# Moving the accumulating weight-sum transfers from the recurrence to the up projections, with new places for casts and low parts

## The chip, the cores and the metric

The kernel runs on one core of a Trainium2 chip. TensorE (PE) multiplies matrices into PSUM, VectorE (DVE) and ScalarE (ACT) do the elementwise work, GpSimd (POOL) does a little of it and issues transfers, SyncE (SP) issues most transfers. Each engine works through its own instructions in order, and waits for the others by semaphores. The metric is the device time of one execution in microseconds (us); the time before is the median of three runs.

## The reference, cut to what matters

A trunk of two layers on 1024 tokens of width 1024, all in float32. Layer 0 mixes tokens by a gated linear recurrence with 8 heads of 128, layer 1 by attention in a window of 128. After each mixer, and after each feed-forward part, comes a layer norm of the residual sum.

```
q, f, i, g = split(h @ w_in, 4)                  # layer 0, per head of 128
fg = lb + (1 - lb) * sigmoid(f)
S_t = diag(fg_t) S_{t-1} + (1 - fg_t) i_t^T ;  o_t = S_t^T silu(q_t)
o = o * rsqrt(mean(o^2) + eps) * g_norm_w * silu(g) ;  mix = o @ w_out
h = layer_norm(alpha * h + mix)
u = causal_depthwise_conv3(h @ ffn_w_in) + conv_b    # both layers, 2 x 2816 columns
a, b = split(u, 2) ;  h = layer_norm(alpha * h + (silu(a) * b) @ ffn_w_out)
```

## The kernel before, in words

**Products.** Every large matrix product is done with operands split into a high part (a cast by ACT to a reduced float32 format) and a low part (what is left, by DVE; `low_part`, L193), in three matmuls of 512 columns (`mm3`, L218 to L220). The largest products are cut into 2 x 2 blocks and done with seven block products instead of eight (numbers 1 to 7 in the code), so that sums and differences of weight blocks are needed beside the weights.

**The order of the work.** `Order` (`od`) keeps an account in us: `od.t` is what PE has been given so far, `od.v` what DVE has. Tasks are Python generators, which `od.tick()` steps when their time in `od.t` has come; `od.fill` lets DVE have one more job as long as `od.v` is under `od.t + od.room`, and `od.hook` issues casts. Costs are guesses written into the calls (`cost=0.03` for a small matmul; `mm3` adds 3 x 512 / 2365 us). In the recurrence the order of PE, SP, ACT, DVE and POOL is the order of these calls (`manual_schedule`). Elsewhere, as in the up projection, only PE's order is so fixed; a planner orders the other engines, each instruction as its operands and its buffer come free, earlier lines first.

**The recurrence** (`recur`, one generator per head). While PE runs the 98 block products of the later heads' q, f, i and g (`product(n)`, L1368 on: 12 matmuls of 512 columns, in four quarters k), the head in hand goes through its levels: DVE updates qp and kp by halves of blocks (`update`, L1083 to L1088), ACT keeps a copy for the next level (`stash`, L1070 and L1071), and PE computes the scores of a level in bursts of small tiles (`scores`, `blocks`, `column_sums`, all L224). Then come transposes of kp and of the values, the states St, the output, and `norm`: squares with sums by ACT (L1197), mean and power by POOL (L1198, L1199), the scaling by DVE into og (L1201), 8 transposes of og by PE (L228).

**Weights in the recurrence.** `raw` tiles are loaded by SP two pairs ahead. For the block products 6 and 7, and 5 and 4, DVE first makes sums in place (jobs "a", L1290 and L1291, and "b", L1293 and L1294). `cast_next` (called by the hook) issues ACT's cast of the next block (L1271) once the sums it needs have been issued to DVE; `job_next` issues DVE's low part at least 1 us of the account after the cast. A block product goes into one of four PSUM banks; before it, the bank's earlier result must have been read (`evacuate`, ACT L1346 to L1352 and DVE L1358).

**Weight sums of the down projections.** Both down projections use four sums of blocks of `ffn_w_out` (`bsd`, in device memory). They are made by transfers alone, issued by POOL: plain copies (L1225) and copies that add to what is there (`accum_op`, L1226). For each layer there are four groups of rows (3, 3, 3 and 2 x 128 of them), of eight transfers each, partly one behind the other; 64 transfers in all. `product(n)` takes one from the list ahead of each of the first 64 block products.

**The start.** x blocks are turned by PE (`x_pair`, L228) and DVE makes sums of their parts (`sums_of_x`, L822 to L825). `last_sums` (L845) casts more of them later.

**Convolution parameters.** `conv_params` waits until 330 in the account, loads them by ACT, has PE turn four pieces (L964), each into a new psax tile (there are two) from which DVE copies (L965).

**The up projection** (`Up.run`). For each of 22 blocks fc of 2 x 128 columns: four loads by SP (L466), casts, sums (L475 to L478) and low parts, seven block products, and `collect`: their sums, the convolution (L521, L523), the gate (L526, L528) and a store to `gd` (L529). The multiplication of L528 is POOL's for fc 0 and 1, DVE's for the rest. The down projection reads `gd`, `ffn_w_out` and, from its third block product on, `bsd`; POOL does the power of each layer norm (L267).

Of the kernel before, what the change touches and what calls it, by code (L numbers as in the profile page):

```python
# [16 lines left out]
P = 128  # L17
# [4 lines left out]
BL = 32  # L22
NH = 8
FF = 2816
NF = FF // P
# [29 lines left out]
class Order:  # L55
# [40 lines left out]
    def tick(self):  # L96
        for task in sorted(self.chains, key=lambda k: k[0]):
            if task[0] <= self.t:
                self.step(task)
        if self.hook:  # L100
            self.hook()
        while self.fill and self.v < self.t + self.room and self.fill():
            pass

    def finish(self, tasks):
# [25 lines left out]
def trunk(ctx: ExitStack, tc: tile.TileContext, a: dict, out: bass.AP):  # L131
    nc = tc.nc
    PS = bass.MemoryType.PSUM
    od = Order()
# [32 lines left out]
    def psax():  # L167
        return axp.tile([P, 1024], F32, name="psax")
# [222 lines left out]
    sub, add = ALU.subtract, ALU.add  # L391
# [7 lines left out]
    class Up:  # L399
# [97 lines left out]
        def collect(self, p, fc, ps):  # L497
# [18 lines left out]
            if p in (4, 3):  # L516
# [10 lines left out]
                else:  # L527
                    (nc.gpsimd if fc < 2 else nc.vector).tensor_tensor(ca, ca, c, op=ALU.mult)  # L528
                    nc.sync.dma_start(gd[:, fc, :], ca)  # L529

        def run(self, ready, down):

            od.finish(ready[:4])
# [12 lines left out]
            for fc in range(2):  # L546
                self.collect(7, fc, self.product(7, fc, mm[2 + fc]))
                self.collect(4, fc, ax[fc])
                self.collect(5, fc, ax[2 + fc])
            self.weights(2)  # L550
            for fc in range(2):
                self.collect(3, fc, self.product(3, fc, mm[fc]))
            banks, n = mm[2:] + ax[:2] + mm[:2] + ax[2:], 0
            for fc in range(2, NF):
                if fc > 2:
                    self.weights(fc)
                for p in (1, 2, 6, 7, 4, 5, 3):
                    self.collect(p, fc, self.product(p, fc, banks[n % 8]))
                    n += 1
                    if fc == NF - 1 and p in (1, 6, 4):  # L560
                        down.ahead.append(down.operands(0, len(down.ahead)))

# [139 lines left out]
    with tc.tile_pool(name="t", bufs=1, reuse_waits="tile") as raws, hgrn_pool as hp:  # L702
# [148 lines left out]
        with tc.tile_pool(name="ep", bufs=1, reuse_waits="tile") as ep:  # L851
# [33 lines left out]
            with tc.manual_schedule(engines={EN.PE, EN.SP, EN.Activation, EN.DVE}):  # L885
# [60 lines left out]
                od.finish([ahead])  # L946
                w0["q"] = qf_split(raws0["q"])
                nc.vector.tensor_copy(msk, mf)
                late = [od.spawn(x_pair(6), 1.0)]

        def conv_params():
            yield 330.0
            for l in range(2):
                crs = []
                for k in range(2):
# [4 lines left out]
                        nc.scalar.dma_start(crs[k][44 * j:44 * (j + 1), :], src.rearrange("(c p) -> c p", p=P))  # L960
                yield 10.0
                for k, cr in enumerate(crs):
                    ps = psax()
                    nc.tensor.transpose(ps[:, :88], cr, ident[:88, :88])  # L964
                    nc.vector.tensor_copy(cwt[:, l, 2 * k:2 * k + 2, :],  # L965
                                          ps[:, :88].rearrange("p (a b) -> p a b", a=2))
                    yield 3.0

            rb = hp.tile([32, 16], F32, name="rb")
            nc.scalar.dma_start(rb, a["rel_bias"])  # L970
# [42 lines left out]
        def recur(h, qs, fg, kp):  # L1013
# [19 lines left out]
            def scores(i, pv, K, Q):  # L1033
# [4 lines left out]
                for c in range(NB):  # L1038
                    for b in range(P // BL):
                        o, g = b * BL, c * (P // BL) + b  # L1040
                        mm32(pv[o:o + BL, c], K[:, g * BL:(g + 1) * BL], second(qv, m)[:, g], cost=0.03,
                             tile_position=(0, o))

                def put():
# [69 lines left out]
            column_sums(sums1, r1, 16)  # L1114
            column_sums(sums2, r2.rearrange("p j b u -> p (j b u)"), 16)
            puts = [scores(2, chunks(ps[:, 384:512]), early, early), scores(3, chunks(ps[:, 768:896]), kp, qp)]
            update(3)
            early = stash(4, hp.tile([P, S], F32, name="kd"))
            place(Ab, 0, chunks(sums0))
# [9 lines left out]
            yield wait  # L1129
            pv = chunks(psax())  # L1130
            low, high = scores(4, pv[:, :, :16], early, early), blocks(5, pv, kp, qp)
            update(5)
            early = stash(6, hp.tile([P, S], F32, name="kd"))
            low()
# [27 lines left out]
            for c in range(NB - 1):  # L1162
                cs = slice(c * P, (c + 1) * P)
                mm32(ps[:, cs], kd[:, cs], V[:, c, :])
            St = hp.tile([P, NB, P], F32, name="St")
            for c in range(NB - 1):
                pc = ps[:, c * P:(c + 1) * P]
# [49 lines left out]
            if h < NH - 2:  # L1217
                nc.sync.dma_start(hod[h], G)

        def weight_sums(l, k0, k1):  # L1220

            w, rows, lower = a["ffn_w_out"][l], slice(k0 * P, k1 * P), slice(FF // 2 + k0 * P, FF // 2 + k1 * P)
            b11, b12, b21, b22 = w[rows, :512], w[rows, 512:], w[lower, :512], w[lower, 512:]
            t1, t2, t3, t4 = [t[rows, :] for t in bsd[l]]
            plain = lambda to, src: lambda: nc.gpsimd.dma_start(to, src)  # L1225
            onto = lambda to, src: lambda: nc.gpsimd.dma_start(to, src, accum_op=add)  # L1226
            return [plain(t3, b22), plain(t1, b11), onto(t3, b12), onto(t1, b12),
                    plain(t2, t3), onto(t2, b11), plain(t4, t2), onto(t4, b21)]

        groups = [weight_sums(l, k0, k1) for l in range(2) for k0, k1 in ((0, 3), (3, 6), (6, 9), (9, 11))]  # L1230
        sums = [one for i in range(0, 8, 4) for four in zip(*groups[i:i + 4]) for one in four]
# [7 lines left out]
        raw_of, landing, cast, low_made, summed_w = {}, {}, {}, set(), set()  # L1239
# [18 lines left out]
        def cast_next(force=False):  # L1258
# [6 lines left out]
                return False  # L1265
            if p in (6, 7) and (m, "a") not in summed_w or p in (5, 4) and (m, "b") not in summed_w:
                return False
            if (m, 0) not in raw_of or p == 3 and (m, 1) not in raw_of or not force and landing[m] > od.t:
                return False
            order_hi.pop(0)  # L1270
# [8 lines left out]
        def job_next(force=False):  # L1279
# [4 lines left out]
            if p in ("a", "b"):  # L1284
# [7 lines left out]
                else:  # L1292
                    tt(b21, b21, b11, op=sub)  # L1293
                    tt(b11, b22, b11, op=sub)  # L1294
                summed_w.add((m, p))
                od.vec(1.4, 0.0)
            else:
                if force:
                    while (m, p) not in cast:
# [69 lines left out]
        def product(n):  # L1369

            m, p = line[n]
            ensure(min(n + 2, len(line) - 1))
            if sums:
                sums.pop(0)()
            b = {2: 1, 5: 2, 3: 2}.get(p, 3 * (m % 2))
            ps = banks[b]
            if b in readers:
# [2 lines left out]
                    od.step(t)  # L1380
            w = home(n)
            for k in range(4):
                mm3(ps, lambda j: w[:, j, k * P:(k + 1) * P], lambda j: moving[p](j, k), k == 0 and p in (1, 2, 5), k == 3, onto=p in (6, 7, 3, 4))
                od.tick()
            done[0] = n + 1
# [42 lines left out]
        with tc.manual_schedule(engines={EN.PE, EN.SP, EN.Activation, EN.DVE, EN.Pool}):  # L1428
# [56 lines left out]
            if sums or jobs or order_hi:  # L1485
# [382 lines left out]
```

## Time and profile before

| | |
|---|---|
| median of 3 runs | 2229.71 us (2228.83 to 2230.94) |
| the profiled execution, its time | 2228.37 us |
| its span, first to last instruction | 2226.6 us |
| PE busy, of the span | 2116.6 us (95%) |
| DVE busy | 1779.9 us (80%) |
| ACT busy | 970.7 us (44%) |
| POOL busy | 185.0 us (8%) |
| mean granted clock of PE | 0.975 |
| transfers by POOL's queue: bytes, share of 16 engines' span | 46.16 MB, 9.8% |
| transfers by SP's queue | 238.26 MB, 32.9% |

The recurrence reaches from about 58 us to 578 us of the span, the first up projection to about 1069 us; the second one ends about 2001 us into it. Busy times are sums over instructions; issuing a transfer or waiting is not counted as busy. The ends of matmuls are modelled, so a busy PE is not PE at its full rate: the granted clock says how fast it was let run, 1.00 being full speed. A row of the timeline gives the start and the length in us, the engine, the line, the operation and its operands (out, then in), and in brackets the idle time ahead of it with what ended it; a row of the waits gives the engine that waited, what it waited for, the total in us, how often, and the longest.

### The profile page before, as it was taken

How to read it: one execution, taken by the hardware profiler on the slowest of the kernel's cores; microseconds unless marked ns; L12 is line 12 of the kernel's file. 1: busy time of each engine (PE TensorE's matmuls, PEld its weight loads, DVE VectorE, ACT ScalarE, POOL GpSimd, SP SyncE). 2: the span in 40 equal slices, each digit the busy share in tenths (PEclk: the TensorE clock that was granted, in tenths of full speed). 3: DMA queues.
4: the chain of work that ended last, by engine and by line, in shares of the span. 5: the costliest groups of instructions: out<-in, count | busy, mean ns of one | idle time of the engine just before them, and what ended most of it. 6: DMA issues, size and time to landing. Idle time of an engine off the chain costs nothing.

```text
span 2226.6 us, 31496 instructions
## 1 busy us (share of the span) xinstructions
PE 2116.6 (95%) x12303; PEld 1759.3 (79%) x12303; DVE 1779.9 (80%) x2422; ACT 970.7 (44%) x1562; POOL 185.0 (8%) x214
## 2 busy tenths in 40 slices
PE   8796978799999999999999999999999999999998
PEld 7675766577777888888888888888888888888887
DVE  5564645567599999998898767897999999988986
ACT  5453444355244444444442336672444444444430
POOL 2012112000011000000000112340100000000001
PEclk9898988899999999999999999999999999999999
DMA  8158878415222322222875441204223222239762
GB/s 271 26 103 204 205 133 201 94 50 169 74 102 85 105 85 78 84 86 95 283 261 189 161 132 34 56 26 155 104 81 99 85 86 85 78 124 308 244 203 107
DMA packets 239789, 286.80 MB, mean 129 GB/s; under 512 B 30184, under 2 KB 160408, under 8 KB 239384
## 3 DMA queue, kind: packets, MB, share of 16 engines
q1 hardware_dynamic: 223328, 238.26, 32.9%
q0 software_dynamic: 15456, 46.16, 9.8%
q8 instruction: 97, 1.59, 0.3%
q10 hardware_dynamic: 856, 0.37, 0.1%
q14 instruction: 52, 0.43, 0.1%
HBM read 241.72 MB, written 89.15 MB: 149 GB/s over the span
## 4 chain that ended last, share of the span: by engine, by line
PE 78%; issue 10%; DVE 5%; DMA 3%; POOL 2%; ACT 2%; SPq 0%; DVEq 0%; POOLq 0%; ACTq 0%
PE psmm L218 15%; PE psmm L220 15%; PE psmm L219 14%; PE psax L218 9%; PE psax L220 9%; PE psax L219 9%; DMA bsd<-bsd 2%; PE psax L224 2%; PE psmm L228 1%; PE psmm L224 1%; PE psax L1642 1%; POOL bsd L1226 1%; PE psax L228 1%; PE psmm L1493 1%; DVE HL L193 0%
## 5 line engine op out<-in xcount | busy, mean ns | idle before, releaser
L218 PE MATMUL psmm<-T,HL 128*128 128x512 f32 x768 | 307.6, 401 | 17.8 <-DVE VG L1358 12.3
L220 PE MATMUL psmm<-T,HL 128*128 128x512 f32 x768 | 302.0, 393 | 3.0 <-DVE HL L193 3.0
L219 PE MATMUL psmm<-T,HL 128*128 128x512 f32 x768 | 301.8, 393 | 0.0
L523 DVE SCALAR_TENSOR_TENSOR Y<-Y,cwt,Y 128x1023 f32<-128x1023 f32 (+1 forms) x176 | 225.2, 1281 | 45.5 <-ACT Y L521 43.9
L245 ACT CAST HL<-rx 128x1024 fp32r<-128x1024 f32 (+1 forms) x151 | 151.6, 1007 | 181.8 <-PE psmm L219 40.2
L193 DVE TENSOR_TENSOR HL<-rx,HL 128x1024 fp32r<-128x1024 f32 (+1 forms) x151 | 176.4, 1174 | 19.3 <-ACT HL L245 19.1
L218 PEld LDWEIGHTS psmm<-T,HL 128*128 128x128 f32 x768 | 146.5, 191 | 48.2 <-DVE VG L1358 12.7
L220 PEld LDWEIGHTS psmm<-T,HL 128*128 128x128 f32 x768 | 145.5, 189 | 35.2 <-DVE HL L193 4.2
L219 PEld LDWEIGHTS psmm<-T,HL 128*128 128x128 f32 x768 | 146.3, 191 | 29.2 <-DVE T L193 0.5
L267 POOL TENSOR_TENSOR rs<-rs,nhalf 128x1 f32<-128x1 f32 x32 | 44.9, 1402 | 1295.5 <-DVE rs L266 1295.4
L521 ACT ACTIVATE Y<-Y,cwt 128x1024 f32<-128x1024 f32 x88 | 108.8, 1237 | 96.1 <-DVE Y L510 85.7
L218 PE MATMUL psax<-T,HL 128*128 128x512 f32 x352 | 137.3, 390 | 0.0
L219 PE MATMUL psax<-T,HL 128*128 128x512 f32 x352 | 137.0, 389 | 0.0
L220 PE MATMUL psax<-T,HL 128*128 128x512 f32 x352 | 136.9, 389 | 0.0
L193 DVE TENSOR_TENSOR HL<-raw,HL 128x512 fp32r<-128x512 f32 (+1 forms) x121 | 93.1, 788 | 31.5 <-ACT HL L1271 18.6
L218 PE MATMUL psmm<-HL 128*128 128x512 f32 x220 | 88.2, 401 | 8.6 <-ACT qs L1348 7.3
L1271 ACT CAST HL<-raw 128x512 fp32r<-128x512 f32 x98 | 55.2, 619 | 91.8 <-DVE raw L1291 62.8
L245 ACT CAST HT<-rx 128x1024 fp32r<-128x1024 f32 (+1 forms) x37 | 35.5, 961 | 127.2 <-DVE rx L477 83.7
L220 PE MATMUL psmm<-HL 128*128 128x512 f32 x220 | 87.1, 396 | 0.0
L219 PE MATMUL psmm<-HL 128*128 128x512 f32 x220 | 87.1, 396 | 0.0
L220 PEld LDWEIGHTS psax<-T,HL 128*128 128x128 f32 x352 | 66.2, 188 | 13.8
L219 PEld LDWEIGHTS psax<-T,HL 128*128 128x128 f32 x352 | 66.1, 188 | 13.6
(392 smaller groups left out, 5393.2 us busy)
## 6 DMA issues: line engine op xcount, KB each, us to landing
rx<-in_ffn_w_in_dram SPq DMA_DIRECT2D x136, 256.0 KB, 3.2
rx<-gd SPq DMA_DIRECT2D x118, 256.0 KB, 3.8
bsd<-in_ffn_w_out_dram POOLq DMA_DIRECT2D x36, 768.0 KB, 7.9
gd<-Y SPq DMA_DIRECT2D x44, 512.0 KB, 2.6
raw<-in_hgrn_w_in_dram SPq DMA_DIRECT2D x30, 512.0 KB, 5.4
rx<-in_ffn_w_out_dram SPq DMA_DIRECT2D x54, 256.0 KB, 4.6
R<-bsd SPq DMA_DIRECT2D x44, 256.0 KB, 5.1
Y<-in_ffn_w_in_dram SPq DMA_DIRECT2D x40, 256.0 KB, 2.9
```

The source lines that it names most:

```text
L193: make = lambda e: e.tensor_tensor(lo, src, hi.bitcast(F32), op=ALU.subtract)
L218: nc.tensor.matmul(ps, st(0), mv(0), start=start, stop=False, skip_group_check=onto)
L219: nc.tensor.matmul(ps, st(0), mv(1), start=False, stop=False, skip_group_check=onto)
L220: nc.tensor.matmul(ps, st(1), mv(0), start=False, stop=stop, skip_group_check=onto)
L224: nc.tensor.matmul(ps, lhsT, rhs, start=start, stop=stop, **kw)
L228: nc.tensor.transpose(ps, src, ident)
L245: nc.scalar.copy(hi, src)
L267: nc.gpsimd.tensor_tensor(rs, rs, nhalf, op=ALU.pow)
L521: nc.scalar.activation(c, u, AF.Identity, bias=cwt[:, l, 3, ci:ci + 1], scale=cwt[:, l, 2, ci:ci + 1])
L523: nc.vector.scalar_tensor_tensor(c[:, sh:], u[:, :S - sh], cwt[:, l, 2 - sh, ci:ci + 1], c[:, sh:], op0=ALU.mult, op1=ALU.add)
L1226: onto = lambda to, src: lambda: nc.gpsimd.dma_start(to, src, accum_op=add)
L1271: nc.scalar.copy(home(n)[:, 0], source(m, p))
```

## The change

- `weight_sums` leaves the recurrence and becomes `sums_of_weights` in `Up`: each layer issues its own 32 transfers in its up projection, two with each fc from 3 on (one where fc is a multiple of 4), two groups of rows interleaved instead of four.
- In the recurrence `od.pour()` issues low parts to DVE (until `od.v` is 0.3 us past `od.t`) right behind a burst of small tiles, in two places ahead of an update and in one ahead of the states.
- `cast_next` no longer issues the casts for block products 6 and 5 before the account says that DVE has made their sums.
- The account: each quarter of a block product counts 0.031 us more, a small tile of `scores` 0.017 us instead of 0.03.
- x blocks 6 and 7 are turned 5 us of the account after their place instead of 1.
- `conv_params` turns all four pieces into one psax tile, allocated at its start and kept to the end of both layers' copies, and copies once per layer.

```diff
+    def pour(self):
+        while self.fill and self.v < self.t + 0.3 and self.fill():
+            pass
...
+        def sums_of_weights(self):
+            def group(k0, k1):
+                w, rows, lower = a["ffn_w_out"][self.l], slice(k0 * P, k1 * P), slice(FF // 2 + k0 * P, FF // 2 + k1 * P)
+                b11, b12, b21, b22 = w[rows, :512], w[rows, 512:], w[lower, :512], w[lower, 512:]
+                t1, t2, t3, t4 = [t[rows, :] for t in bsd[self.l]]
+                plain = lambda to, src: lambda: nc.gpsimd.dma_start(to, src)
+                onto = lambda to, src: lambda: nc.gpsimd.dma_start(to, src, accum_op=add)
+                return [plain(t3, b22), plain(t1, b11), onto(t3, b12), onto(t1, b12),
+                        plain(t2, t3), onto(t2, b11), plain(t4, t2), onto(t4, b21)]
+            groups = [group(*k) for k in ((0, 3), (3, 6), (6, 9), (9, 11))]
+            return [one for i in (0, 2) for two in zip(*groups[i:i + 2]) for one in two]
...
             for fc in range(2, NF):
                 if fc > 2:
                     self.weights(fc)
+                for _ in range(2 if fc % 4 else 1):
+                    if sums and fc > 2:
+                        sums.pop(0)()
                 for p in (1, 2, 6, 7, 4, 5, 3):
...
-                late = [od.spawn(x_pair(6), 1.0)]
+                late = [od.spawn(x_pair(6), 5.0)]
...
             yield 330.0
+            ps = psax()
...
                 for k, cr in enumerate(crs):
-                    ps = psax()
-                    nc.tensor.transpose(ps[:, :88], cr, ident[:88, :88])
-                    nc.vector.tensor_copy(cwt[:, l, 2 * k:2 * k + 2, :],
-                                          ps[:, :88].rearrange("p (a b) -> p a b", a=2))
-                    yield 3.0
+                    nc.tensor.transpose(ps[:, 512 * l + 88 * k:512 * l + 88 * k + 88], cr, ident[:88, :88])
+                yield 1.0
+                nc.vector.tensor_copy(cwt[:, l].rearrange("p (k a) b -> p k (a b)", k=2),
+                                      ps[:, 512 * l:512 * l + 176].rearrange("p (k x) -> p k x", k=2))
+                yield 1.0
...
-                        mm32(pv[o:o + BL, c], K[:, g * BL:(g + 1) * BL], second(qv, m)[:, g], cost=0.03,
+                        mm32(pv[o:o + BL, c], K[:, g * BL:(g + 1) * BL], second(qv, m)[:, g], cost=0.017,
...
             puts = [scores(2, chunks(ps[:, 384:512]), early, early), scores(3, chunks(ps[:, 768:896]), kp, qp)]
+            od.pour()
             update(3)
...
             low, high = scores(4, pv[:, :, :16], early, early), blocks(5, pv, kp, qp)
+            od.pour()
             update(5)
...
                 mm32(ps[:, cs], kd[:, cs], V[:, c, :])
+            od.pour()
             St = hp.tile([P, NB, P], F32, name="St")
...
             if p in (6, 7) and (m, "a") not in summed_w or p in (5, 4) and (m, "b") not in summed_w:
                 return False
+            if not force and p in (6, 5) and summed_w[m, "a" if p == 6 else "b"] > od.t:
+                return False
...
-                summed_w.add((m, p))
                 od.vec(1.4, 0.0)
+                summed_w[m, p] = od.v + 0.2
...
             ensure(min(n + 2, len(line) - 1))
-            if sums:
-                sums.pop(0)()
...
             for k in range(4):
+                od.t += 0.031
                 mm3(ps, lambda j: w[:, j, k * P:(k + 1) * P], lambda j: moving[p](j, k), k == 0 and p in (1, 2, 5), k == 3, onto=p in (6, 7, 3, 4))
```

More of the change, by code (lines that the diff above doesn't have):

```diff
@@ L529, in collect @@
                     nc.sync.dma_start(gd[:, fc, :], ca)
+        def sums_of_weights(self):
[9 more added lines that the diff above has]
+            return [one for i in (0, 2) for two in zip(*groups[i:i + 2]) for one in two]
         def run(self, ready, down):
+            sums = self.sums_of_weights()
             od.finish(ready[:4])
@@ L559, in run @@
                     n += 1
+                    if fc == NF - 1 and p == 1 and sums:
+                        raise ValueError("a sum is left")
                     if fc == NF - 1 and p in (1, 6, 4):
@@ L1218, in norm @@
                 nc.sync.dma_start(hod[h], G)
[L1220 to L1231, printed above, removed]
         SEQ = (1, 2, 6, 5, 7, 3, 4)
@@ L1238, in trunk @@
         place_of = {mp: n for n, mp in enumerate(line)}
-        raw_of, landing, cast, low_made, summed_w = {}, {}, {}, set(), set()
+        raw_of, landing, cast, low_made, summed_w = {}, {}, {}, set(), {}
         done, opened = [0], [0]
@@ L1484, in trunk @@
             moved.append(od.spawn(move(6, 1, 1, VG[6][:, 1, 512:], 1.0)))
-            if sums or jobs or order_hi:
+            if jobs or order_hi:
                 raise ValueError("something is left")
```

## The prediction, made before the result was known

> **What bounds the kernel now.** I read the page first, then all that TensorE (PE) waited for, then each of the longest waits in the timeline of every engine, then the granted clock behind them. The span is
>
> ```profile
> span 2226.6 us, 31496 instructions
> ```
>
> and the run took 2228.37 us, 1.3 us under the median 2229.71 of the three runs. PE is busy almost throughout, so only its idle time and its slow clock can be won. The waits of PE (total, times, longest):
>
> ```profile
> PE psax L228 <- DVE og L1201: 33.2, 2, 19.5
> PE psmm L218 <- DVE VG L1358: 12.3, 1, 12.3
> PE psmm L218 <- ACT qs L1350: 11.4, 3, 4.2
> PE psmm L218 <- ACT qs L1348: 7.3, 3, 3.8
> PE psmm L218 <- ACT fg L1346: 5.7, 1, 5.7
> PE psmm L218 <- ACT T L845: 5.5, 1, 5.5
> PE psax L228 <- issue: 5.1, 2, 4.0
> PE psax L964 <- DVE cwt L965: 3.1, 1, 3.1
> ```
>
> The first two rows are three stops in the recurrence. The timeline of POOL, ACT, DVE and PE around the longest (start, length, what, idle before):
>
> ```profile
> 207.82 0.88 POOL L1226 DMA_DIRECT2D bsd<-in_ffn_w_out_dram  x1 [6.49 <-issue]
> ...
> 209.57 1.67 POOL L1199 TENSOR_TENSOR ss<-ss,nhalf 128x8 f32<-128x8 f32 x1
> ...
> 182.68 0.19 ACT L1197 ACTIVATION_READ_ACCUMULATOR sq<-psax 128x1 f32 x1
> ...
> 187.68 0.68 DVE L1358 TENSOR_TENSOR VG<-VG,psmm 128x512 f32<-128x512 f32 x1
> 211.27 1.23 DVE L1201 TENSOR_TENSOR og<-psax,ss 128x1024 f32<-128x1024 f32 x1 [22.90 <-POOL ss L1199]
> ...
> 212.55 1.97 PE L228 MATMUL psax<-ident,og 128*128 128x128 f32 x8 [19.52 <-DVE og L1201]
> ```
>
> ACT had the sums of squares at 182.87, but POOL took the power (L1199) only at 209.57: it stands behind adding transfers (L1226) that POOL cannot issue until earlier ones have moved on. DVE and ACT, in order as well, stand behind it, and PE with them. The other two stops, before 339.64 (13.7 us, the rest of the row of og) and before 414.53 (12.3, L1358, which stands behind og on DVE), are alike. The stretches after the three (columns: length; PE, PEld, DVE, ACT, POOL busy; granted clock; DMA share, GB/s) run at half the clock; the first row is the recurrence from its second head on:
>
> ```profile
> 110.00:500.00 390.00, 323.02 (x3080) 265.38 (x3078) 232.94 (x419) 171.74 (x370) 54.83 (x66) 0.90 0.63 141
> ...
> 212.55:215.96 3.41, 3.41 (x12) 3.09 (x13) 3.38 (x6) 2.11 (x4) 0.49 (x1) 0.51 1.36 469
> 339.64:345.64 6.00, 6.00 (x19) 5.06 (x19) 5.97 (x10) 3.45 (x6) 1.00 (x1) 0.50 1.01 389
> 414.53:420.67 6.14, 6.14 (x18) 5.07 (x19) 6.11 (x10) 2.15 (x4) 0.00 (x0) 0.50 0.05 8
> ```
>
> **The change part by part.** *Transfers out of the recurrence.* All 64 leave POOL's queue there; left are the two small operations of each norm (L1198, L1199). Without the queue, the power would start at 182.9 and end before 185; DVE could take og when it is through with L1358, at 188.4, and be done at 189.6; PE stopped at 212.55 - 19.52 = 193.0, so nothing of the stop is left. The three stops give 33.2 + 12.3 = 45.5 us. The half-clock stretches give 3.41 x 0.49 + 6.00 x 0.50 + 6.14 x 0.50 = 7.7 us. Together 53.2. [...]
>
> A second count: from head to head, by the transposes of og,
>
> ```profile
> 138.54 1.04 PE L228 MATMUL psax<-ident,og 128*128 128x128 f32 x8
> ...
> 473.86 1.03 PE L228 MATMUL psax<-ident,og 128*128 128x128 f32 x8
> ...
> 528.70 1.03 PE L228 MATMUL psax<-ident,og 128*128 128x128 f32 x8
> ```
>
> six heads take 390.2 us, and the last, with no transfer left, 54.8. Six of these would be 329, 61 less. So this term lies between 53 and 61; I take 53, since the three stops are seen one by one.
>
> *Transfers into the up projections* (32 in each, one or two with each of fc 3 to 21). On POOL they pass the multiplications of fc 0 and 1 (L528) and stand ahead of the down projection's norms (L267); nothing of the up projection waits for POOL after fc 1. On SP's queue only the down projection's loads of the sums wait for them, and the first of these comes two whole products in. What they take of POOL's time is read from the recurrence:
>
> ```profile
> 9.61 1.22 POOL L1225 DMA_DIRECT2D bsd<-in_ffn_w_out_dram  x2
> ...
> 128.25 0.73 POOL L1198 TENSOR_SCALAR ss<-ss 128x8 f32<-128x8 f32 x1 [76.65 <-ACT sq L1197]
> ...
> 409.72 0.88 POOL L1226 DMA_DIRECT2D bsd<-in_ffn_w_out_dram  x1 [7.42 <-issue]
> ```
>
> (409.72 - 9.61 - 76.65) / 63 = 5.1 us apiece (between the first and the last of 64, less the wait in the middle row): 164 us per layer, in a stretch of over 310 us, shown here by its row. What hides them is the lead of the weight loads:
>
> ```profile
> 700.00:1010.00 310.00, 306.50 (x1340) 253.27 (x1340) 283.54 (x313) 133.74 (x147) 5.67 (x2) 0.99 0.27 89
> ...
> 807.30 0.92 SPq L466 DMA_DIRECT2D Y<-in_ffn_w_in_dram  x2
> ...
> 829.70 0.62 ACT L245 CAST HL<-Y 128x512 fp32r<-128x512 f32 x1 [1.66 <-PE psmm L219]
> ...
> rx<-in_ffn_w_in_dram SPq DMA_DIRECT2D x136, 256.0 KB, 3.2
> ```
>
> The DMA engines are 27% busy there, a load lands in 3.2 us and (here into Y) is read 22.4 us after its issue, so 19 us more would cost nothing. If that cover goes, PE (306.5 of 310 busy) stops at once. I take 0; bounds 0 and a loss of 6, should a few loads come late.
>
> *Casts of sums later.* ACT is in order too:
>
> ```profile
> 82.79 0.62 ACT L1271 CAST HL<-raw 128x512 fp32r<-128x512 f32 x1 [4.97 <-DVE raw L1294]
> ...
> 83.83 0.58 ACT L1346 COPY fg<-psmm 128x512 f32<-128x512 f32 x1
> ...
> 84.46:89.80 5.34, 5.34 (x16) 3.85 (x17) 1.29 (x2) 2.55 (x5) 0.00 (x0) 0.52 0.00 0
> ```
>
> The cast of a sum that DVE had not made held up the emptying of a bank, PE waited 5.7 us (row L1346 above) and ran 5.34 us at 0.52, together 8.2. With the cast held back until the sum is due, the copy goes first. The casts behind it in the list are held back too, and a low part that needs one may come late: between 0 and 8.2, taken as 6, since PE was already waiting for the copy.
>
> *Low parts in the bursts, and a truer account* (0.031 us more per quarter of a product, 0.017 for 0.03 per small tile: no instruction). DVE idles while PE runs a burst, and later has low parts ahead of an update for which ACT waits:
>
> ```profile
> DVE qp L1083 <- PE psax L224: 17.4, 8, 4.8
> ...
> 226.21 0.71 DVE L193 TENSOR_TENSOR HL<-raw,HL 128x512 fp32r<-128x512 f32 x1
> ...
> 227.43 0.68 DVE L193 TENSOR_TENSOR HL<-raw,HL 128x512 fp32r<-128x512 f32 x1
> 228.03 0.69 DVE L1083 TENSOR_TENSOR qp<-qp,tot 128x512 f32<-128x512 f32 x1
> ```
>
> A burst's idle time of 2.2 us holds both low parts (1.4 us); the update comes 1.2 us earlier, ACT's copies after it too, and the 6 waits of L1348 and L1350 (18.7 us) shrink by as much: 7, and 1 for a clock that no longer drops. Bounds: all 18.7 with some 10 of slow clock (6 times the 1.7 us that the first stretch above lost), and a loss of 10, where the new account issues bursts before DVE has their operands and low parts stand in front of an update. I take 8. The wait for T (5.5, row L845) comes from the same backlog of ACT: I leave it as it is, bounds 0 and 7 (with 1.7 of slow clock).
>
> *Parameters in one tile:* the 3.1 us wait for L965 goes; but one of the two psax tiles is held through both layers' loads, so a burst may wait for the other: between 4 gained and 6 lost, taken as 3.
>
> *Start:* x blocks 6 and 7 are turned 4 us later in the account, and no transfer shares the first 45 us with their loads:
>
> ```profile
> 35.47 1.94 PE L228 MATMUL psax<-ident,Y 128*128 128x128 f32 x8 [3.96 <-issue]
> ```
>
> Of 5.1 us of waits I take 4; bounds 0 and 6.5 with the clock. Sixteen transposes, two splits and the sums of two blocks move together.
>
> The sum: 53 + 0 + 6 + 8 + 3 + 4 = 74 us. On the profiled run 2154; on the median **2156**. All good ends give 61 + 8 + 29 + 7 + 4 + 6.5 = 115, so 2114; the poor ones 53 - 6 + 0 - 10 - 6 + 0 = 31, so 2199.
>
> **The rivals.** *The transfers come forward again: slower.* POOL's order is written by hand in the recurrence, but not in the up projection, where a planner lays an instruction wherever its operands are there. The trace shows how far: a load that the code has in the down projection runs before stores of the up projection,
>
> ```profile
> 1033.66 0.32 SPq L687 DMA_DIRECT2D Y<-ynd  x1
> ...
> 1064.80 0.32 SPq L529 DMA_DIRECT2D gd<-Y  x1
> ```
>
> and that one waited for a buffer; the transfers wait for none. Placed at the start, 64 of them hold POOL until 10 + 64 x 5.1 = 336, while the first norm needs it at 128: PE stands some 208 us, less my 74: 2229.7 + 134 = 2364. It decides from (128 - 10) / 5.1 = 23 transfers ahead of the first norm on; were the planner's account of transfers right, it would come out near 2230, the change not doing what it says. Against it: the instructions seen to move forward did so by tens of microseconds, this needs hundreds. 0.16, of which 0.03 for near 2230.
>
> *The up projection becomes the bound.* [...] In rows: it decides where a load takes over 22.4 us; two transfers wholly ahead of it, landing as slowly as the copies of sums in the page's list,
>
> ```profile
> bsd<-bsd POOLq DMA_DIRECT2D x12, 768.0 KB, 9.5
> ```
>
> and its own 3.2 make 2 x 9.5 + 3.2 = 22.2, the edge. One us late in each of the 38 fc of two layers: 2156 + 38 = 2194. Against it: 27% busy. 0.05.
>
> *The waits trade places.* Freed of POOL, each of 7 heads meets one more wait for ACT of 4.2 us and 2 of slow clock, and nothing else is won: 2229.7 - 53 + 44 = 2221. For it: ACT's queue already ends the third to sixth row of PE's waits. 0.07.
>
> **How the numbers follow.** Forecast 0.72. A measurement tells 0.2%, 4.5 us, from no change. Faster: 0.72 + 0.07 + 0.05 = 0.84; same 0.03; slower 0.13. The forecast's own range is 2114 to 2199; 2112 to 2206 takes in the up projection as well and leaves out the first rival and the third.
>
> **What would show it.** POOL's rows in the recurrence hold L1198 and L1199 alone, the power starts within 1 us of the last square, and no PE wait for og or VG L1358 exceeds 2 us; the granted clock of 110 to 500 rises from 0.90; head to head is 50 to 56 us. In the up projection the DMA share rises from 0.27 to about 0.5 with PE as busy as before. Wrong would be: transfers (bsd) on POOL before 600 us; waits of ACT for L466 loads in the up projection; more or longer waits for L1346 to L1350.

## The result: 2359.1 us, slower, and the profile after

The median of four runs is 2359.1 us (2358.3 to 2361.06), beside 2229.27 us of four runs of the kernel before: a ratio of 1.0583, 95% interval 1.0564 to 1.0601. The profiled execution took 2359.76 us, with a span of 2357.7.

What PE waited for comes first (total, times, longest), to be held beside the eight rows shown of before:

```profile
PE psax L232 <- DVE og L1229: 206.7, 2, 206.4
PE psmm L222 <- ACT qs L1365: 6.5, 5, 1.3
...
PE psmm L222 <- ACT T L869: 5.5, 1, 5.5
...
PE psmm L222 <- ACT fg L1363: 3.9, 1, 3.9
PE psmm L222 <- ACT qs L1367: 3.6, 1, 3.6
PE psax L228 <- issue: 3.0, 2, 2.4
```

Three stops of 19.5, 13.7 and 12.3 us have become one of 206.4. Lines have moved: L222, L228 and L232 are L218, L224 and L228 of before. So the last row is small tiles (L224 of before) and not the turning of x, whose wait for "issue" (5.1 us, L228 of before) is gone, as is the one for cwt. The rows of qs and fg have shrunk, that of T has stayed. It is again og that PE waits for, and og waits for POOL. POOL's own timeline from the start past the first norm (of the 64 transfers the first few and the last are shown):

```profile
8.01 2.37 POOL L197 TENSOR_TENSOR HL<-raw,HL 128x1024 fp32r<-128x1024 f32 x1 [3.17 <-DVE HL L798]
10.34 1.22 POOL L541 DMA_DIRECT2D bsd<-in_ffn_w_out_dram  x2
18.69 0.60 POOL L541 DMA_DIRECT2D bsd<-in_ffn_w_out_dram  x1 [7.14 <-issue]
...
31.15 1.05 POOL L542 DMA_DIRECT2D bsd<-in_ffn_w_out_dram  x1 [6.63 <-issue]
...
336.75 0.90 POOL L542 DMA_DIRECT2D bsd<-in_ffn_w_out_dram  x1 [7.20 <-issue]
337.73 0.19 POOL L1226 TENSOR_SCALAR ss<-ss 128x8 f32<-128x8 f32 x1
338.00 1.69 POOL L1227 TENSOR_TENSOR ss<-ss,nhalf 128x8 f32<-128x8 f32 x1
388.34 0.71 POOL L1226 TENSOR_SCALAR ss<-ss 128x8 f32<-128x8 f32 x1 [48.65 <-ACT sq L1225]
```

L541 and L542 are the transfers that the code has in the up projections. Not one of them runs there: all 64, those of layer 1 too, stand ahead of the first norm, one each (336.75 - 10.34) / 63 = 5.18 us, with POOL mostly idle on "issue" between them, which names nothing that it waited for. The times do: wherever POOL idles like this behind a transfer that adds (L542), the next starts 0.25 to 0.38 us after that one has landed (31.15 + 7.5 = 38.65 us for the one shown, the next at 38.95). The first norm's mean, L1226, has no idle time in front of it: it starts as the last transfer is out. From the second norm on POOL waits for ACT, as it should. The timeline of all engines, first where ACT ends the eighth square, then where POOL is through:

```profile
125.25 0.19 ACT L1225 ACTIVATION_READ_ACCUMULATOR sq<-psax 128x1 f32 x1
125.69 0.96 POOL L542 DMA_DIRECT2D bsd<-in_ffn_w_out_dram  x1 [6.96 <-issue]
...
339.72 1.23 DVE L1229 TENSOR_TENSOR og<-og,ss 128x1024 f32<-128x1024 f32 x1 [208.57 <-POOL ss L1227]
...
341.00 1.97 PE L232 MATMUL psax<-ident,og 128*128 128x128 f32 x8 [206.36 <-DVE og L1229]
341.58 0.62 ACT L1095 COPY VG<-qp 128x512 f32<-128x512 f32 x1 [215.17 <-DVE qp L1108]
```

ACT had the squares at 125.44; the power came 212.6 us later. DVE's og waited 208.6 us, and behind it DVE's updates, ACT's copies and PE. The windows (length; PE, PEld, DVE, ACT, POOL busy; granted clock; DMA share, GB/s) show the stop, the stretch behind it, and 390 us of recurrence after it:

```profile
135.00:341.00 206.00, 0.00 (x0) 0.00 (x0) 1.28 (x2) 0.00 (x0) 32.72 (x43) 0.51 0.70 145
341.00:348.00 7.00, 7.00 (x24) 5.93 (x25) 6.96 (x13) 4.48 (x7) 0.00 (x0) 0.61 0.31 98
342.00:732.00 390.00, 376.61 (x3676) 311.06 (x3675) 279.60 (x497) 203.65 (x427) 18.51 (x14) 0.99 0.23 73
```

Once the transfers are out of the way PE is busy 376.6 of 390 us at a clock of 0.99; before it was 323.0 of 390 at 0.90. So the gain that the forecast counted is there, some 77 us of it (2229.3 - 2359.1 + 206.4 = 76.6), and a stop of 206 us stands on top.

### The profile page after: what moved, and what is told of

Same layout as the page of the kernel before. It is cut to its first block, busy times and chain, and to the rows that moved or that the text cites. A ratio compares the mean times of both kernels' runs of the same rounds, so it can differ in the third digit from the quotient of the medians.

```text
span 2357.7 us, 31500 instructions
## 1 busy us (share of the span) xinstructions
PE 2100.8 (89%) x12303; PEld 1747.0 (74%) x12303; DVE 1778.9 (75%) x2420; ACT 971.1 (41%) x1562; POOL 187.7 (8%) x214
## 4 chain that ended last, share of the span: by engine, by line
PE 79%; issue 11%; DVE 3%; POOL 2%; DMA 2%; ACT 1%; SPq 0%; ACTq 0%; DVEq 0%; POOLq 0%
PE psmm L222 15%; PE psmm L224 15%; PE psmm L223 15%; PE psax L222 8%; PE psax L224 8%; PE psax L223 8%; PE psax L228 3%; PE psmm L232 1%; PE psmm L228 1%; POOL bsd L542 1%; PE psax L1658 1%; PE psax L232 1%; DMA bsd<-bsd 1%; PE psmm L1509 1%; POOL bsd L541 1%
## 5 line engine op out<-in xcount | busy, mean ns | idle before, releaser
L222 PE MATMUL psmm<-T,HL 128*128 128x512 f32 x768 | 305.8, 398 | 5.5 <-ACT T L869 5.5
L224 PE MATMUL psmm<-T,HL 128*128 128x512 f32 x768 | 301.4, 393 | 2.4 <-DVE HL L197 2.4
L232 PE MATMUL psax<-ident,og 128*128 128x128 f32 x64 | 9.3, 292 | 206.7 <-DVE og L1229 206.7
L197 DVE TENSOR_TENSOR HL<-rx,HL 128x1024 fp32r<-128x1024 f32 (+1 forms) x151 | 176.3, 1174 | 18.7 <-ACT HL L249 18.5
L222 PEld LDWEIGHTS psmm<-T,HL 128*128 128x128 f32 x768 | 145.6, 190 | 34.8 <-ACT T L869 5.6
L224 PEld LDWEIGHTS psmm<-T,HL 128*128 128x128 f32 x768 | 145.3, 189 | 34.1 <-DVE HL L197 3.2
L232 PEld LDWEIGHTS psax<-ident,og 128*128 128x128 f32 x64 | 8.0, 150 | 208.3 <-DVE og L1229 207.5
L1229 DVE TENSOR_TENSOR og<-og,ss 128x1024 f32<-128x1024 f32 x1 | 1.2, 1226 | 208.6 <-POOL ss L1227 208.6
L222 PE MATMUL psax<-T,HL 128*128 128x512 f32 x352 | 137.3, 390 | 0.0
L224 PE MATMUL psax<-T,HL 128*128 128x512 f32 x352 | 137.0, 389 | 0.0
L197 DVE TENSOR_TENSOR HL<-raw,HL 128x512 fp32r<-128x512 f32 (+1 forms) x121 | 91.8, 787 | 24.9 <-ACT HL L1288 13.7
L222 PE MATMUL psmm<-HL 128*128 128x512 f32 x220 | 87.2, 396 | 7.8 <-ACT qs L1365 6.5
L224 PE MATMUL psmm<-HL 128*128 128x512 f32 x220 | 85.8, 390 | 0.0
```

What stands on the lines that cost most here:

```text
L197: make = lambda e: e.tensor_tensor(lo, src, hi.bitcast(F32), op=ALU.subtract)
L222: nc.tensor.matmul(ps, st(0), mv(0), start=start, stop=False, skip_group_check=onto)
L224: nc.tensor.matmul(ps, st(1), mv(0), start=False, stop=stop, skip_group_check=onto)
L232: nc.tensor.transpose(ps, src, ident)
```

## The experiments

Theory A: the transfers stand ahead of the first norm in POOL's in-order queue, and only their number there sets the stop. Theory B: the up projection could not bear them. Theory C: it is their traffic, not their place in the queue. Each time below is the median of four or five runs, and each ratio is to the kernel before, run beside it (medians of 2227.7 to 2229.2 us).

**The transfers held in the up projection.** POOL's multiplication of fc 1 is remembered, and each transfer ordered behind it (the held kernel, below):

```
-                    (nc.gpsimd if fc < 2 else nc.vector).tensor_tensor(ca, ca, c, op=ALU.mult)
+                    self.made = (nc.gpsimd if fc < 2 else nc.vector).tensor_tensor(ca, ca, c, op=ALU.mult)
+                    self.held = self.made if fc < 2 else self.held
...
                     if sums and fc > 2:
-                        sums.pop(0)()
+                        with tc.issue_after(self.held.ins):
+                            sums.pop(0)()
```

> All edits of the change, with one addition: each transfer of the sums is ordered behind POOL's multiplication of fc 1 in its own up projection, so it cannot be laid ahead of it. Theory A (POOL's queue: the 64 transfers ahead of the first norm's power make PE's stop of 206.4 us): the stop goes whole, 2359.1 - 206.4 = 2153, between 2145 and 2165, and POOL holds the two operations of each norm alone until 600 us. Theory B (the up projection cannot bear the transfers): the stop goes, but 1 us or more is late in each of 38 fc, 2190 or more, with PE waiting for casts of the up projection's loads.

2148.66 us (2146.5 to 2150.09), ratio 0.9634, interval 0.9617 to 0.9652. The stop is gone whole: 2359.1 - 2148.7 = 210.4, of which 206.4 are the stop and 2.7 its half clock (5.4 us at 0.50, last section). POOL's timeline of this kernel, the first norms and layer 0's transfers:

```profile
123.55 0.73 POOL L1228 TENSOR_SCALAR ss<-ss 128x8 f32<-128x8 f32 x1 [113.77 <-ACT sq L1227]
124.36 2.13 POOL L1229 TENSOR_TENSOR ss<-ss,nhalf 128x8 f32<-128x8 f32 x1
176.95 0.71 POOL L1228 TENSOR_SCALAR ss<-ss 128x8 f32<-128x8 f32 x1 [50.45 <-ACT sq L1227]
...
630.98 1.32 POOL L542 DMA_DIRECT2D bsd<-in_ffn_w_out_dram  x2
...
810.72 0.90 POOL L543 DMA_DIRECT2D bsd<-in_ffn_w_out_dram  x1 [9.35 <-issue]
```

And its windows: the recurrence, then layer 0's and layer 1's up projection for as long as the transfers run (layer 1's from 1569.29 to 1747.61 us, all but the last of them inside the window):

```profile
110.00:500.00 390.00, 374.79 (x3694) 309.74 (x3693) 277.55 (x491) 206.64 (x445) 21.37 (x16) 1.00 0.21 68
...
630.00:811.00 181.00, 176.47 (x770) 145.04 (x769) 164.06 (x184) 75.88 (x87) 24.61 (x33) 0.99 0.88 215
...
1569.00:1741.00 172.00, 172.00 (x760) 142.42 (x760) 162.39 (x182) 73.86 (x84) 23.65 (x32) 1.00 0.90 219
```

In layer 1 PE is busy 172 of 172 us at full clock while the transfers run, with a DMA share of 0.90; the kernel before, in the same window and without them, has a share of 0.28. In layer 0 PE is busy 176.5 of 181 us, and 177.0 in the run with the norms off POOL (below), which has no transfer there. The weight loads do get slower, but not by as much as the lead of 22.4 us that the prediction read. Into rx they land in 3.2 us in layer 1's window before, and in the held kernel in 5.7 (the last number):

```profile
rx<-in_ffn_w_in_dram SPq DMA_DIRECT2D x30, 256.0 KB, 5.7
```

ACT waits 12 us for such loads in that window (6 before), and PE not at all. Theory B falls with this. In this kernel the 32 transfers go in a row, and not one or two with each fc as the change has them. **Spread over the fc** (each transfer waits for DVE's last multiplication of the fc before, instead of `issue_after`):

> As pinned, but each transfer waits for DVE's last multiplication of the fc before its own, so that one or two go with each fc from 3 on, as the change describes it, instead of all 32 in a row as the ring takes them. Forecast: nothing in the up projection waits for POOL, the same time as pinned within 4 us, 2145 to 2153. Rival (bursts of transfers cost the up projection something): 4 us or more faster than pinned.

2147.14 us, ratio 0.9636 (0.9623 to 0.9649): no difference that can be told from the transfers in a row. From 640 to 985 us, where layer 0's transfers now run, PE is busy all 345 us at a DMA share of 0.61.

**How many are ahead.** Only layer 0's transfers are left free, all 32 of them or the first 20; the rest are held as above (for 20 the condition has `and len(sums) > 12` too):

```
-                    if sums and fc > 2:
+                    if sums and fc > 2 and self.l == 0:
+                        sums.pop(0)()
+                    elif sums and fc > 2:
                         with tc.issue_after(self.held.ins):
```

> As the pinned kernel for layer 1, but layer 0's 32 transfers are free to go ahead. Theory A: they hold POOL until 10 + 32 x 5.2 = 176 us, the first norm asks at about 131, so PE has one stop of some 45 us: 2153 + 45 = 2198, between 2190 and 2215. If the count of transfers ahead did not set the stop (theory C, or a stop from another cause), the time would be near 2359 or near 2153.

> As the run with layer 0's 32 transfers ahead (one stop of 45.6 us), but only 20 of them are free to go ahead; the other 12 are pinned in the up projection. Theory A: POOL is free at 10 + 20 x 5.2 = 114 us, ahead of the first norm at 124 to 131, so there is no stop (the forecast's rival put the point at 23): 2149 to 2158, the upper part for the traffic. A theory by which any transfer ahead of the norms holds them up would give 20/32 of the 50 us: 2180.

With 32 ahead 2198.82 us, ratio 0.986 (0.9841 to 0.9879); with 20 ahead 2150.6 us, ratio 0.965 (0.9637 to 0.9664). What PE waited for with 32 ahead, and POOL at the end of them:

```profile
PE psax L232 <- DVE og L1233: 45.6, 2, 45.3
```

```profile
175.90 0.92 POOL L543 DMA_DIRECT2D bsd<-in_ffn_w_out_dram  x1 [7.95 <-issue]
176.90 0.19 POOL L1230 TENSOR_SCALAR ss<-ss 128x8 f32<-128x8 f32 x1
```

With 20 ahead POOL is done at 110 and waits for ACT:

```profile
109.43 0.97 POOL L543 DMA_DIRECT2D bsd<-in_ffn_w_out_dram  x1 [8.62 <-issue]
124.17 0.73 POOL L1230 TENSOR_SCALAR ss<-ss 128x8 f32<-128x8 f32 x1 [13.77 <-ACT sq L1229]
```

The stop begins where the queue is longer than the time to the first norm: 20 transfers end 14 us early and cost nothing measurable, 32 end 51 us late and cost 50.

**The norms taken off POOL.** The transfers stay ahead, and the heads' scaling goes to DVE; the power is left out, so og has other values.

```
-            nc.gpsimd.tensor_scalar(ss, ss, 1.0 / P, RMS_EPS, op0=ALU.mult, op1=ALU.add)
-            nc.gpsimd.tensor_tensor(ss, ss, nhalf.to_broadcast([P, NB]), op=ALU.pow)
+            nc.vector.tensor_scalar(ss, ss, 1.0 / P, RMS_EPS, op0=ALU.mult, op1=ALU.add)
```

> The changed kernel with its 64 transfers where they are (from 10 to 337 us on POOL), but the heads' norms ask nothing of POOL: the scaling goes to DVE and the power is left out, so the norms' factors are not those of the reference. Theory A (order on POOL alone): no stop is left, 2145 to 2165 although the DMA engines carry the transfers beside the recurrence. Theory C (the transfers' traffic, a DMA share of 0.70 in the first 340 us, is what holds the recurrence): weight loads come late, PE waits for casts of raw, 2200 or more.

2163.12 us, ratio 0.9698 (0.9679 to 0.9717): no stop, but 14.5 us over the kernel with the transfers held. Whether that is traffic or the scaling on DVE was open, so the same edit went into the held kernel:

> The pinned kernel with the heads' scaling on DVE and the power left out (the norms' factors are not those of the reference), as in the run with the transfers ahead, which took 2163.1. If the 14 us by which that was over the pinned kernel are the price of the transfers' traffic beside the recurrence, this takes 2148 as the pinned one, or less; if they are the price of eight more operations in DVE's queue that wait for ACT's squares, this takes about 2163.

2161.0 us, ratio 0.9691 (0.9678 to 0.9704). So it is the scaling on DVE, 12.3 us, and the traffic makes no difference that can be told (2163.1 beside 2161.0). DVE now stands in front of ACT's squares, as expected:

```profile
DVE ss L1228 <- ACT sq L1227: 30.8, 6, 6.0
```

The windows of the two, transfers ahead and then held:

```profile
110.00:500.00 390.00, 369.75 (x3643) 304.25 (x3643) 273.84 (x492) 205.66 (x440) 33.63 (x44) 0.98 0.61 149
```

```profile
110.00:500.00 390.00, 370.25 (x3638) 304.78 (x3636) 273.62 (x491) 204.69 (x438) 0.00 (x0) 0.98 0.21 68
```

A DMA share of 0.61 instead of 0.21 leaves PE's busy time where it is. Theory C falls.

**The move alone** (the held transfers, every other edit of the change undone):

> The kernel before with one edit alone: its 64 transfers go behind POOL's multiplication of fc 1 in the two up projections. By the three stops and their half-clock stretches it gains 53, by the heads' distances 61: 2168 to 2176. If the waits trade places (each of 7 heads meets one more wait for ACT), it gains only about 10: 2220.

2172.46 us, ratio 0.9742 (0.9721 to 0.9763): 56.7 us for the transfers, 23.8 for all the rest. POOL's first and seventh norm now start at 130.45 and 460.05, 54.9 us from head to head, where the forecast's second count had 54.8. The rest was then undone edit by edit in the held kernel (the edits in short):

```
no pour:     -            od.pour()                                     (three places)
no account:  -                od.t += 0.031        and  cost=0.017 -> 0.03
no casts:    -            if not force and p in (6, 5) and summed_w[...] > od.t: return False
no start:    x_pair(6), 5.0 -> 1.0
no conv:     the two loops over four psax tiles of the kernel before
```

> The pinned kernel (2148.7 us) without the three pours of low parts into the bursts of small tiles. Theory P (the forecast's term of 8 us for pours and account is mostly the pours: DVE's low parts stand ahead of an update that ACT and PE wait for): 5 to 8 us more, 2154 to 2157, PE's waits for ACT qs longer again (in the pinned kernel 6.5 in 5 and 3.6 in 1). Rival: the account alone brings the waits down, and without the pours the time stays within 3 us of 2148.7.

> The pinned kernel with the old account (no 0.031 per quarter of a product, 0.03 per small tile again); no instruction is another, only their order. Theory P: within 3 us of 2148.7. Rival (the account is what places ACT's and DVE's work rightly): 5 us or more slower, with the casts and copies of the heads in another order. The forecast's bounds for both edits together were 29 gained and 10 lost.

> The pinned kernel without the pours and with the old account. Undone alone, the pours cost 18 us (2166.9) and the account 12 (2161.0); the forecast gave both together 8. If they add up: 2148.7 + 30 = 2179, more than the kernel with the move alone (2172.5) has; if each needs the other: about 2166 to 2168, which leaves some 8 us for the start and nothing for casts and parameters (2172.5 - 2148.7 = 23.8 = 16 + 8).

2166.87 us without the pours (ratio 0.9722, 0.9709 to 0.9735), 2161.04 without the account (0.9697, 0.9683 to 0.971), 2164.46 without either (0.9709, 0.9696 to 0.9722). The first two are more than the 5 to 8 and the under 3 us that were expected. Each alone costs about what both cost: they work as a pair, worth 15.8 us. PE's waits, held kernel first, then without the pours:

```profile
PE psmm L222 <- ACT qs L1367: 6.5, 5, 1.3
...
PE psmm L222 <- ACT qs L1369: 3.6, 1, 3.6
```

```profile
PE psmm L222 <- ACT qs L1366: 11.9, 3, 4.3
PE psmm L222 <- ACT qs L1364: 8.8, 3, 3.0
```

The two waits for qs, 20.7 us without the pours, are 10.1 with them; the clock of 110 to 500 is 0.96 without, 1.00 with. Without both edits these waits are 16.6 us (11.8 and 4.8), and the window is

```profile
110.00:500.00 390.00, 370.03 (x3628) 305.43 (x3627) 274.77 (x486) 203.36 (x428) 19.07 (x14) 0.97 0.21 68
```

> The pinned kernel in which the casts of sums may again go before DVE has made the sum. The forecast's term: the one wait of PE for fg of 5.7 us with its half clock comes back, 6 us more (between 0 and 8.2): 2155. In the pinned kernel a wait for fg of 3.9 us is left, so a rival holds that only 5.7 - 3.9 = 1.8 us and little clock were won: 2148 to 2151.

> The pinned kernel with x blocks 6 and 7 turned as early in the account as before (1.0 in place of 5.0). The forecast's term: PE waits again for Y at 35 us, 4 us more (0 to 6.5): 2153. Rival: with no transfer beside the loads of x the blocks are there in time anyway, within 2 us of 2148.7; against it, the kernel with the move alone kept a wait of 3.4 us there (4.5 in two), without a transfer of the sums in that stretch.

> The pinned kernel with the convolution's parameters in four psax tiles as before. The forecast's term: PE's wait for cwt of about 3 us comes back, 3 us more (between 6 less and 4 more): 2152. Rival: the wait comes back but the two tiles held no longer give it back elsewhere, within 2 us of 2148.7.

Without the casts' condition 2146.83 us (0.9639, 0.9625 to 0.9652) and with the parameters in four tiles 2146.93 (0.9633, 0.9619 to 0.9646): neither edit does anything that can be told. With the early turn of x 2156.76 (0.9678, 0.9665 to 0.9691), 8.1 us more, and a wait that the held kernel does not have is back in PE's timeline:

```profile
34.48 1.06 PE L232 MATMUL psax<-ident,Y 128*128 128x128 f32 x8 [3.41 <-issue]
```

**Why the casts' condition did nothing.** The row of fg, 3.9 us long, is the same with it (at 79 us) and without (at 81). In ACT's order the copy of fg still stands behind a cast that waits 4.4 us for DVE's sum:

```profile
77.93 0.62 ACT L1290 CAST HL<-raw 128x512 fp32r<-128x512 f32 x1 [4.38 <-DVE raw L1313]
78.45 0.58 ACT L1365 COPY fg<-psmm 128x512 f32<-128x512 f32 x1
```

In the code the new condition begins with `not force`; at the first two products of the first pair `ensure` wants the low parts of two products ahead, whose sums and casts are not there yet, and forces them. What did change this wait is the pair of pours and account: with the condition in force throughout, it is 5.7 us without both, 3.9 with both or with the account alone, and 0.6 with the pours alone. To see what the order on ACT is worth, it was changed directly, by issuing the copy ahead of `ensure`, and then the casts for T in one go:

```
             m, p = line[n]
+            if m == 0 and p == 2:
+                od.step(evacs[0][0])
             ensure(min(n + 2, len(line) - 1))
```

> The pinned kernel with one copy moved: the emptying of the first product's bank of the first pair (fg, for which PE still waits 3.9 us at 79) is issued ahead of the casts that the program forces at the second product. Theory F (the edit of the casts did nothing at this place, because there the sum and the cast behind it are forced, and the new condition does not hold for forced casts): the wait for fg goes, with its half clock, 3.9 + 2 = 6 us less, 2143. Rival (the casts are late because DVE is late, and the next product needs them anyway): the wait moves to a cast of raw or to T, within 2 us of 2148.7.

> As copy_first, and the four casts of the sums of x's first half (T, for which PE waits 5.5 us at 90) are issued together instead of one by one between DVE's operations. If ACT's order alone is at fault: another 5.5 us and some 2 of slow clock, 2143 - 7 = 2136. Rival: T's low parts on DVE come as late as the casts did, or the copies of qs behind them wait longer, and the time stays at that of copy_first.

2145.29 us (0.9626, 0.9612 to 0.9639) and 2144.91 us (0.9623, 0.961 to 0.9636): 3.4 and 3.8 us below the held kernel, with intervals that overlap its own. PE's waits in its timeline from 70 to 100 us in the held kernel, with the copy first, and with copy and casts first:

```profile
79.09 0.50 PE L222 MATMUL psmm<-Y,HL 128*128 128x512 f32 x1 [3.89 <-ACT fg L1365]
90.35 0.80 PE L222 MATMUL psmm<-T,HL 128*128 128x512 f32 x1 [5.48 <-ACT T L871]
```

```profile
87.03 0.79 PE L222 MATMUL psmm<-T,HL 128*128 128x512 f32 x1 [7.37 <-ACT T L871]
```

```profile
83.48 0.79 PE L223 MATMUL psmm<-T,HL 128*128 128x512 f32 x1 [6.22 <-DVE T L197]
```

The wait for fg goes as theory F had it, but part of it moves on: to T's cast, and with the casts early to T's low parts on DVE. Of 9.4 us of waits 2 are won by the copy and 3 by both. What ends the wait that is left is DVE, so DVE is what is late in this stretch. The first run's time lies between theory F (6 us less) and its rival (within 2 us); for the second the rival was right.

## Why the prediction was wrong, point by point

**The step that failed** is the heading of the second term, "Transfers into the up projections (32 in each, one or two with each of fc 3 to 21)". It took the place of the transfers from the code. In the program none of them is there: they need no buffer and no operand but, some of them, one another, and the planner lays them at the front. The code has the room for it: in the start (L909) the order written by hand names PE, SP, ACT and DVE but not POOL, and all 64 stand behind POOL's last operation of the start (L197, at 8.01) and ahead of its first of the recurrence (L1226). Why the planner chooses the front is not shown by a run; that nothing else held the transfers is, since one order edge for each keeps them in the up projection. Transfers (bsd) on POOL before 600 us are what the prediction itself had named as a sign of being wrong. The first rival had this, with its price, 2364 beside a measured 2359.1: POOL held until 336 (the last transfer is out at 337.7), a stop of 208 (206.4), the point of decision at 23 transfers (20 cost nothing, 32 cost 50 us). It got 0.16, for the reason "the instructions seen to move forward did so by tens of microseconds, this needs hundreds". That reason was bad. The load that moved by tens waited, by the prediction's own words a few sentences earlier, for a buffer, so its row need not show how far the planner reaches with an instruction that waits for none. Layer 1's transfers, which run from 1569 us on when they are held, moved forward by over 1200 us.

**The term that was to be won** was right. 53 us (53 to 61) were predicted for the three stops and their clock, 56.7 measured with the move alone. The up projection bears the transfers at no cost: 0 predicted, PE busy 172 of 172 us. The DMA share is 0.61 with the transfers spread, where about 0.5 was expected, and 0.90 with them in a row. The lead of the weight loads, 22.4 us, was a sound reason: their landing grew only from 3.2 to 5.7 us.

**Casts of sums later:** 6 predicted, nothing measured. "With the cast held back until the sum is due, the copy goes first" is the failed step: the cast that PE waited behind was a forced one, which the condition excepts. The row of the trace told which wait it was, but not by which of two paths the cast had been issued; the code did.

**Pours and account:** 8 predicted, 15.8 measured, within the bounds of -10 and 29. The mechanism was right: the two edits take the waits for qs from 16.6 to 10.1 us, 6.5 where the forecast had 7. The clock was the undersized part: between 110 and 500 us it is 0.97 without both edits and 1.00 with them, some 11 us of 370 busy ones, where the forecast gave it 1. The two windows agree with that: 374.8 x 1.00 - 370.0 x 0.97 is 16 us of PE's work at full speed, waits and clock together.

**Parameters in one tile:** 3 predicted, nothing that can be told measured. **Start:** 4 predicted, 8.1 measured, above the bound of 6.5; the wait of 3.4 us with a clock of 0.97 in place of 1.00 in the first 58 us accounts for about 5, and the two profiled spans differ by no more (2152.6 and 2147.8); the rest of the medians' distance is not followed up.

**The sum** of the terms as measured is 56.7 + 0 + 0 + 15.8 + 0 + 8.1 = 80.6, and the held kernel is 80.5 under before. That they meet to 0.1 us is luck, since the medians of kernels that cannot be told apart lie some 2 us from each other (2146.8 to 2148.7). 74 was predicted, as 2156; 2147.1, with the transfers spread over the fc, is what the change takes when it does what it says. That 74 is so near 80 is luck in part too: 9 us too much for casts and parameters stand against 16 too little for the stops, the pair and the start. **The other rivals:** the waits did not trade places (the rows of qs, the third and fourth of before, fell), and the up projection did not become the bound: that a load waits out two whole transfers and lands after 22.2 us was an estimate, and beside the transfers the loads into rx landed in 5.7 us (median).

## What to carry to other kernels

Where a scheduler orders an engine, an instruction's line says nothing about when it runs: ask for each moved instruction what holds it back, and if nothing does (no operand of another engine, no buffer, no instruction ahead of it in a written order), cost it at the front of its queue, with everything that queue has to do for others. The test is a count: so many instructions by their pace, against the time at which the queue is first needed. Order edges behind one instruction of the intended stage turned a loss of 130 us into a gain of 80.

## What the runs showed of the hardware that was not expected

The queue of these transfers went at much the same pace in both places: 5.18 us apiece ahead of the recurrence, (810.72 - 630.98) / 31 = 5.8 in a row in layer 0's up projection. Traffic at a DMA share of 0.61 beside the recurrence cost it nothing that could be told (2163.1 beside 2161.0 us), and at 0.90 beside layer 1's up projection PE did not stop; what a transfer costs here is its place in the queue. Beside the transfers, which POOL issues, weight loads from SP landed in 5.7 us instead of 3.2; the issuing engine's own order mattered far more, a stop of 206.4 us.

The clock after the long stop is seen in the lengths of PE's matmuls of 512 columns:

```profile
342.62 0.78 PE L222 MATMUL psmm<-T,HL 128*128 128x512 f32 x1
343.20 0.63 PE L223 MATMUL psmm<-T,HL 128*128 128x512 f32 x1
...
345.76 0.63 PE L223 MATMUL psmm<-T,HL 128*128 128x512 f32 x1
346.19 0.49 PE L224 MATMUL psmm<-T,HL 128*128 128x512 f32 x1
346.52 0.39 PE L222 MATMUL psmm<-T,HL 128*128 128x512 f32 x1
```

They take 0.63 us until about 346.4 and 0.39 after, so full speed comes 5.4 us after PE starts again at 341.00 (granted clock 0.50 from there to 346.40, 1.00 from 346.40 to 350). The first 1.6 us of these are the eight transposes. The half-clock stretches of before were 3.41, 6.00 and 6.14 us, behind stops of 19.5, 13.7 and 12.3: the stop of 206 us cost no more of it than one of 12.
